# A two-layer hybrid decoder trunk: the first modulation in eight blocks instead of four, constants in three transfers, tiles 4 to 7 modulated in pairs

## The chip, the cores and the metric

The kernel runs on one core of a Trainium2 chip. The metric is the device time of one execution in microseconds (us). The engines are named as in the profile: PE is TensorE, ACT is ScalarE, DVE is VectorE, POOL is GpSimd, SP is SyncE, whose queue issues most of the DMAs. In the timeline an engine's name with a q (SPq) means that the row is an issue.

## The reference

```python
def hybrid_layer(x, c_act, ...):                       # x: 1024 tokens x 1024, two layers
    mod = c_act @ w_mod + b_mod                        # one row of 3072
    shift, scale, gate = jnp.split(mod[:, None, :], 3, axis=-1)
    h = rms_norm(x, pre_gain) * (1.0 + scale) + shift
    proj = h @ w_in                                    # 3088 columns
    (aq, ak, av, ag, rq, rk, rv, rg, gq, gk, gv, gg, ga) = jnp.split(proj, IN_SPLITS, axis=-1)
    ...                                                # windowed attention, retention, gated linear attention
    y = jnp.concatenate([a_out, r_out, g_out], axis=-1) @ w_out
    return x + gate * rms_norm(y, post_gain)
```

with `c_act = silu(c)`. What matters here is the start of layer 0: `shift` and `scale` are sums over 1024 rows of an 8 MB part of `w_mod`, every normalised token row is scaled by `gain = pre_gain * (1 + scale)` and moved by `shift`, and only then can the first projection begin.

## The kernel before

The tokens are 8 tiles of 128. `hT[(l, p)]` holds the modulated, transposed activations of the pair p of tiles in two halves of an fp32 value (a high part, rounded to fp32r, and the remainder), so each projection is three passes: high by high, high by low, low by high. Weights are split in the same way: a `Paced` load has `issue()` (a DMA of 256 KB into one of five stage buffers `st`) and `convert()` (high part on ACT, low part on POOL or DVE). The places of weights and activations lie in two areas, `arena0` and `arena1`.

`first_stage` is written out by hand, and all five engines follow its order (`manual_schedule`). It does the following for tiles 0 to 3:

- It loads `c`, the identity `ident`, `freq` (frequencies for the rotary tables), the bias rows, the four x tiles `xe`, and `w_m0`, the part of `w_mod` for shift and scale, into `wm` in the space of `arena1`, together with the first projection weights `gg` and `rg`.
- It normalises each tile: sum of squares on ACT (L731), scale and power on DVE and POOL (`rstd_of`, L604, L607), scaling on DVE (L745). `tables` is a chain of DVE steps for the rotary tables, of which `more(n)` places the next n.
- `spin(n)` issues n matmuls of the identity by itself, whose result is not used.
- In each of 4 rounds s, two blocks of 128 features are handled. `turn(s)` transposes the two blocks of the four tiles into two PSUM banks and sums 8 chunks of `wm[:, s]` weighted with `c_act` into the bank `pm`, on four 32-row strips. ACT copies the sums (`row`, L782), four small matmuls with `sel` add the strips and turn them into columns of `pc`, DVE makes `gain` and `shift` (L790 to L792), ACT modulates one block and DVE the other (L799 to L803), and DVE takes the remainders (L806).
- `products(s - 1, ...)` multiplies the blocks of the round before by `gg`, 24 matmuls of 272 columns into the four accumulators `acc`; some of them stand ahead of the columns of round s, the rest behind the modulation.
- After the last round come `rg`'s four conversions, into `arena1`, and the 24 products of blocks 6 and 7. Then x of tiles 4 to 7 is loaded in half tiles into buffers `kept`.

Everything after is ordered by a planner for PE: jobs (generators) yield delays from the table `L` or flags, the clock `clk` counts an estimated cost of each matmul, and `pump()` steps the jobs that are due between chunks of projection matmuls. The other engines' orders are set by when their instructions are recorded. Tiles 4 to 7 are jobs of `pre_first`, one for each tile: after the delays `pf3` and `pf2` they take squares (L621), scale (L637), wait `pre1`, and then for each half tile transpose four blocks into an `aux` bank, modulate each with its own instruction of 128 columns (L651 on ACT, L653 on DVE), and split (L657, L658). The projections `rg` of tiles 0 to 3 run meanwhile (`mm` banks); tanh copies of the gates are L1079, and the low-rank gate inputs of the gated linear attention are transposed one tile at a time and copied by L1097.

There are 3 PSUM banks with the tag `mm` and 5 with the tag `aux`; the four `acc` and `pm` hold the five.

Of the kernel before, what the change touches and what calls it, by code (L numbers as in the profile page):

```python
# [10 lines left out]
F32 = mybir.dt.float32  # L11
# [49 lines left out]
def host_constants():  # L61
    f = np.float32
    c = {}
    c["ident"] = np.eye(P, dtype=f)
# [4 lines left out]
    c["freq"] = np.broadcast_to(freq, (P, 64)).copy()  # L69
    c["causal"] = (i[:, None] <= i[None, :]).astype(f)  # L70
    c["mask2"] = ((i[:, None] <= i[None, :]) & (i[:, None] // 32 == i[None, :] // 32)).astype(np.int32)
    c["curmask"] = (i[:, None] >= i[None, :]).astype(np.int32)
    gam = 1.0 - 2.0 ** (-5.0 - np.arange(4, dtype=np.float64))
    c["reps"] = (4.0 * EPS * gam[None, :] ** (-2.0 * (i[:, None] + 1.0))).astype(f)
    c["vdec"] = (gam[None, :] ** (-(i[:, None] + 1.0))).astype(f)
# [4 lines left out]
    c["cdt"] = cdt  # L80
    c["ones"] = np.ones((P, 4), f)
    r = np.ones((P, 256), f)
    r[:, ::32] = 0.0
    c["rmask"] = r
    c["hmask"] = (i[:, None] // 32 == np.arange(4)[None, :]).astype(f)
# [8 lines left out]
def trunk(ctx: ExitStack, tc: tile.TileContext, ins, cst, out):  # L94
# [153 lines left out]
    ident = cload("ident", eng=A)  # L248
# [227 lines left out]
    def load(l, name, first=None):  # L476
# [10 lines left out]
        def conv(kc, st):  # L487
# [5 lines left out]
            else:  # L493
# [4 lines left out]
                e = G if first == "AG" or name[0] == "o" and kc == 2 else eng(f"wlo{kc}")  # L498
# [125 lines left out]
    def pre(l, t, xt, xn=None):  # L624
# [7 lines left out]
        xn = xn or junk  # L632
# [28 lines left out]
    def pre_first(t, xt):  # L661
        yield L["pf3"] + L["pf2"] * (t - 4)
        yield from pre(0, t, xt, xt)
# [10 lines left out]
    def first_stage():  # L674
# [3 lines left out]
        freq = cload("freq", eng=A)  # L678
# [10 lines left out]
        wm = bp.tile([P, 4 * SLOT], F32, tag="arena1", name="wm").rearrange("p (s k n) -> p s k n", s=4, k=KT)  # L689
        gg, rg = load(0, "gg", "AG"), load(0, "rg", "AV")  # L690

        def wm_load(s):
            for i in range(2):
                nc.sync.dma_start(wm[:, s, 4 * i:4 * i + 4], w_m0[s, :, 4 * i:4 * i + 4])

        for s in range(3):
            gg.issue()
            wm_load(s)
# [18 lines left out]
        spin(6)  # L717
        V.tensor_copy(posf, pr[:, 0:8])
        more(3)
        A.activation(th0, c_nat, AF.Tanh, scale=0.5)  # L720
        V.scalar_tensor_tensor(c_act, th0, 1.0, c_nat, ALU.add, ALU.mult)
        V.tensor_scalar(c_act, c_act, 0.5, None, ALU.mult)
        pr = mm()
        transp(pr[:, 0:24], rows, ident[0:24, 0:24])
        spin(18)
        rc = small(24)
        base = small(8)
        sel = small(1)
        for t in range(4):
            ss = small(1)  # L730
            A.activation(wm[:, 3, 2 * (t % 2):2 * (t % 2) + 2].rearrange("p k n -> p (k n)"), xe[t], AF.Square, accum_out=ss)  # L731
            r = rstd_of(ss, 1, 1.0 / D, EPS)
            if t == 0:
                more(1)
            elif t == 1:
                V.tensor_copy(rc, pr[:, 0:24])
                V.tensor_scalar(base, rc[:, 8:16], 1.0, None, ALU.add)
                V.tensor_reduce(sel, ident[:, 0:97:32], AX.X, ALU.add)
                more(1)
            elif t == 2:  # L740
                more(1)
            else:
                A.activation(w[:, 0, :, 256:272], low, AF.Copy)
                V.tensor_tensor(w[:, 1, :, 256:272], low, f(w[:, 0, :, 256:272]), ALU.subtract)
            V.tensor_scalar(xe[t], xe[t], r, None, ALU.mult)  # L745
        gg.convert()
        gg.issue()
        wm_load(3)
        for _ in range(4):
            rg.issue()  # L750
        for p in range(2):
            hT[(0, p)] = place(TOK[0][p])

        def product(t, b, x, y, start, stop):
            h = hT[(0, t // 2)]
            mult(acc[t][:, 0:272], h[:, x, b, (t % 2) * P:(t % 2) * P + P], w[:, y, b, 0:272], start, stop)

        def products(s, ts):
            for t in ts:
                for b in (2 * s, 2 * s + 1):  # L760
                    for x, y in ((0, 0), (0, 1), (1, 0)):
# [1081 lines left out]
```

## Time and profile before

| | us |
|---|---|
| median of 3 runs (984.5 to 988.84) | 985.13 |
| the profiled execution | 987.97 |
| its span, first to last instruction | 986.0 |
| PE busy in the span | 963.0 |
| DVE, ACT, POOL busy | 682.5, 396.2, 246.2 |
| mean granted clock of PE | 0.993 |

A row of a stretch (`10.00:20.00 ...`) gives its length, then for each of PE, PEld, DVE, ACT and POOL the busy time with the number of instructions, then the granted PE clock (1.00 is full), the share of the DMA engines and GB/s. A stretch asked for PE alone has only PE's busy time. A row of the timeline gives the start, the length, the engine, the line of the kernel, the operation, destination and sources with their shapes, how many follow each other, and in brackets how long the engine stood idle before it and what released it. A matmul of fp32 data is two records, one of fp32r data is one; so 16 records of 128x512 in `aux<-wm,c_act` are 8 sums, and 8 records of `mm<-sm,t` are 4 columns.

### The profile page before, as it was taken

Reading aid. Unit: us, or ns where it says so; the run is one execution under the profiler, and the core shown is the slowest. Engines: PE = TensorE matmul, PEld = TensorE weight load, DVE = VectorE, ACT = ScalarE, POOL = GpSimd, SP = SyncE. Lnnn points to the kernel's source line nnn. Section 1 sums busy time; section 2 is a strip of 40 time slices with the busy share of each in tenths; the row PEclk is TensorE's granted clock in tenths of the full one; section 3 lists DMA queues with packets and bytes.
Section 4 is the critical chain, followed back from the end, with each engine's and each line's share of the span. In section 5 each row is a group of like instructions: output and inputs, shape, how many; then the busy total and the mean of one; then the engine's idle time right before and its main releaser. Section 6 shows DMA issues by size and latency. Waiting matters only on the chain. (4 is left out here: it accounts for less than half of the span.)

```text
span 986.0 us, 19571 instructions
## 1 busy us (share of the span) xinstructions
PE 963.0 (98%) x7184; PEld 830.4 (84%) x7184; DVE 682.5 (69%) x1602; ACT 396.2 (40%) x1114; POOL 246.2 (25%) x310
## 2 busy tenths in 40 slices
PE   6999999999999999999999999999999999999996
PEld 4789999989997777778889999998999877777775
DVE  6476868777766787754697376785765577676885
ACT  3475301233322656633365321133333256664231
POOL 2321101233320324420124010123322034545000
PEclk9999999999999999999999999999999999999999
DMA  9745614542225254597665131352122334488783
GB/s 347 272 118 164 220 33 140 154 125 92 86 85 153 92 182 156 161 299 238 211 201 177 49 97 39 112 147 69 52 96 86 129 91 124 121 264 278 247 269 125
DMA packets 108735, 150.33 MB, mean 152 GB/s; under 512 B 12088, under 2 KB 59740, under 8 KB 107616
## 3 DMA queue, kind: packets, MB, share of 16 engines
q1 hardware_dynamic: 97200, 134.75, 43.4%
q10 hardware_dynamic: 11440, 14.34, 4.0%
q8 instruction: 56, 0.92, 0.4%
q14 instruction: 39, 0.32, 0.1%
HBM read 110.25 MB, written 36.70 MB: 149 GB/s over the span
## 5 line engine op out<-in xcount | busy, mean ns | idle before, releaser
L172 PE MATMUL mm<-arena,arena 128*128 128x256 f32 (+2 forms) x1824 | 298.7, 317 | 0.5 <-DVE t L1260 0.3
L172 PE MATMUL mm<-arena 128*128 128x256 f32 (+2 forms) x1728 | 284.8, 318 | 0.0
L172 PEld LDWEIGHTS mm<-arena,arena 128*128 128x128 f32 x1824 | 253.5, 190 | 26.1 <-issue 4.8
L172 PEld LDWEIGHTS mm<-arena 128*128 128x128 f32 x1728 | 240.4, 189 | 24.3 <-issue 4.2
L607 POOL TENSOR_TENSOR sm<-sm,mhalf 128x1 f32<-128x1 f32 (+1 forms) x64 | 57.6, 900 | 295.0 <-DVE sm L604 159.1
L172 PE MATMUL mm<-arena,mx 128*128 128x512 f32 (+1 forms) x564 | 130.9, 388 | 0.3 <-DVE t L1461 0.3
L172 PEld LDWEIGHTS mm<-arena,mx 128*128 128x128 f32 x564 | 101.5, 188 | 24.5 <-issue 1.5
L156 ACT ACTIVATE t<-aux 128x256 f32<-128x256 f32 (+2 forms) x124 | 52.4, 437 | 94.7 <-PE aux L187 78.2
L156 ACT ACTIVATE arena<-st 128x512 fp32r<-128x512 f32 x94 | 56.2, 628 | 47.5 <-PE mm L172 19.2
L499 POOL TENSOR_TENSOR arena<-st,arena 128x512 fp32r<-128x512 f32 x31 | 44.9, 1448 | 106.8 <-ACT arena L156 60.9
L1018 POOL TENSOR_TENSOR smx<-smx,sm 128x512 f32<-128x512 f32 x32 | 35.0, 1095 | 132.7 <-DVE sm L1017 115.9
L499 DVE TENSOR_TENSOR arena<-st,arena 128x512 fp32r<-128x512 f32 x77 | 61.5, 821 | 5.3 <-ACT arena L156 3.7
L1014 ACT ACTIVATE smx<-smx,sm 128x129 f32<-128x129 f32 x128 | 49.9, 393 | 31.3 <-DVE sm L1011 31.3
L318 DVE SCALAR_TENSOR_TENSOR acc<-ms,c_act,acc 128x512 f32<-128x512 f32 x60 | 46.3, 772 | 14.8 <-DMA ms<-in_w_mod_dram 14.1
L1062 ACT ACTIVATE t<-aux 128x256 f32<-128x256 f32 x32 | 12.2, 382 | 77.6 <-PE aux L172 70.2
L172 PEld LDWEIGHTS aux<-t,mx 32*128 32x128 f32 (+1 forms) x896 | 39.8, 187 | 3.8 <-issue 1.7
L172 PE MATMUL aux<-t,mx 32*128 32x32 f32 (+1 forms) x896 | 40.9, 272 | 0.0
L1009 DVE COPY_PREDICATED smx<-c_curmask,aux 128x256 f32<-128x256 int32 x64 | 25.2, 445 | 17.4 <-ACT smx L156 14.8
L1364 DVE SCALAR_TENSOR_TENSOR t<-t,sm,t 128x512 f32<-128x512 f32 x32 | 24.3, 781 | 18.2 <-DMA t<-in_x_dram 8.7
L187 PE MATMUL aux<-c_ident,t 128*128 128x128 f32 x186 | 32.9, 277 | 1.5 <-ACT t L1194 0.9
L172 PEld LDWEIGHTS aux<-kT,mx 64*128 64x128 f32 x384 | 24.6, 185 | 10.9 <-issue 6.3
L1067 DVE TENSOR_TENSOR t<-aux,sm 128x256 f32<-128x256 f32 x32 | 13.6, 425 | 27.3 <-POOL sm L607 27.3
(260 smaller groups left out, 1431.7 us busy)
## 6 DMA issues: line engine op xcount, KB each, us to landing
st<-in_w_in_dram SPq DMA_DIRECT2D x96, 256.0 KB, 3.7
ms<-in_w_mod_dram SPq DMA_DIRECT2D x64, 256.0 KB, 3.7
mx<-mixS SPq DMA_DIRECT2D x20, 512.0 KB, 5.4
st<-in_w_last_dram SPq DMA_DIRECT2D x36, 256.0 KB, 3.4
wm<-in_w_m_dram SPq DMA_DIRECT2D x8, 1024.0 KB, 11.3
mixS<-t SPq DMA_DIRECT2D x40, 128.0 KB, 2.0
t<-in_x_dram SPq DMA_DIRECT2D x18, 256.0 KB, 5.1
mixS<-t ACTq DMA_DIRECT2D x32, 128.0 KB, 2.1
```

Of the source, the lines that this page charges most:

```text
L156: A.activation(dst, src, AF.Copy)
L172: T.matmul(dst, lhsT, rhs, start=start, stop=stop)
L187: T.transpose(dst, src, idn)
L318: V.scalar_tensor_tensor(acc, wt, c_act[:, k:k + 1], acc, ALU.mult, ALU.add)
L499: e.tensor_tensor(lo, st, f(hi), ALU.subtract)
L607: G.tensor_tensor(r, r, mhalf[:, :w], ALU.pow)
L1009: V.copy_predicated(sv, curmask.unsqueeze(1).to_broadcast((P, 2, P)), pv[:, :, n // P - 1, :])
L1014: A.activation(sm[:, h, :], sm[:, h, :], AF.Exp, bias=mx[:, h:h + 1], accum_out=sums[:, h:h + 1])
L1018: eng("pn").tensor_tensor(sm[:, :, 0:128], sm[:, :, 0:128], rs.unsqueeze(2).to_broadcast((P, 4, P)), ALU.mult)
L1062: A.activation(sq, po, AF.Square)
L1067: V.tensor_tensor(h4(g1), h4(po), r.unsqueeze(2).to_broadcast((P, 4, 64)), ALU.mult)
L1364: V.scalar_tensor_tensor(xt[j], yg[j], r, xt[j], ALU.mult, ALU.add)
```

## The change

- **Constants.** `ident` and `freq` come as one transfer `early`; the nine later constants as two, `late` and `masks`; the small gate weights with 4 transfers instead of 8.
- **First stage.** `w_m0` is laid out in 8 blocks of 128 features (256 columns, shift and scale) and loaded a block at a time, one block ahead of the first `gg` load. Each of 8 rounds b sums 256 columns into one half of `pm`, transposes block b + 1, makes two columns, `gain` and `shift` of one block with two DVE instructions, and modulates the block (ACT in even rounds, DVE in odd ones, both in the last). In round b the products of block b - 1 stand behind everything else. `gg` is converted in even rounds, the `rg` loads are issued in rounds 0 and 2, two of `rg`'s conversions move ahead of the last modulation. The spins are 8 and 12 instead of 6, 18 and 6; the table steps are spread anew.
- **Tiles 4 to 7.** `norm` takes the squares and scales; it runs for tiles 4 and 5 at the end of `first_stage`. `pre_pair` handles two tiles at a time: in each of four steps two blocks of both tiles go into one bank, are modulated with instructions of 256 columns (DVE in even steps, ACT in odd ones) and split for the pair. The table `L` gets `pf4@2`, `pf4@3`, `pf5` and a new `pf3`.
- The low part of two of `rg`'s chunks goes to POOL instead of DVE.

On DVE, around the norms of tiles 0 to 3, before (`mx_141` is the table chain's buffer, `xk` and `mx_107` are the x tiles, the `sm` are small columns):

```order
L718 COPY sm_92<-mm_132 128x8
L364 TENSOR_TENSOR mx_141<-sm_92,c_freq 128x512
L367 TENSOR_SCALAR mx_141<-mx_141 128x512
L369 TENSOR_SCALAR mx_141<-mx_141 128x512
L721 SCALAR_TENSOR_TENSOR c_act<-sm_79,sm_72 128x8
L722 TENSOR_SCALAR c_act<-c_act 128x8
L604 TENSOR_SCALAR sm_173<-sm_171 128x1
L372 SCALAR_TENSOR_TENSOR mx_141<-mx_141 128x512
L745 TENSOR_SCALAR xk_105<-xk_105,sm_173 128x1024
L604 TENSOR_SCALAR sm_180<-sm_178 128x1
```

and after:

```order
L750 COPY sm_92<-mm_129 128x8
L363 TENSOR_TENSOR mx_141<-sm_92,c_early 128x512
L366 TENSOR_SCALAR mx_141<-mx_141 128x512
L368 TENSOR_SCALAR mx_141<-mx_141 128x512
L753 SCALAR_TENSOR_TENSOR c_act<-sm_79,sm_72 128x8
L754 TENSOR_SCALAR c_act<-c_act 128x8
L371 SCALAR_TENSOR_TENSOR mx_141<-mx_141 128x512 x2
L762 TENSOR_REDUCE sm_165<-c_early 128x1
L603 TENSOR_SCALAR sm_169<-sm_167 128x1
L371 SCALAR_TENSOR_TENSOR mx_141<-mx_141 128x512
L772 TENSOR_SCALAR xk_103<-xk_103,sm_169 128x1024
L603 TENSOR_SCALAR sm_176<-sm_174 128x1
```

The first table step reads `c_early` in place of `c_freq`, and two more table steps stand ahead of the first norm.

On PE, one round of before (the third; `mm_332` and `mm_333` take the transposes, `mm_217` is `pc`, `aux_125` to `aux_128` are the accumulators):

```order
L187 MATMUL mm_332<-c_ident,mx_107 128x128 x2
L187 MATMUL mm_333<-c_ident,xk_105 128x128
L187 MATMUL mm_333<-c_ident,xk_106 128x128
L187 MATMUL mm_333<-c_ident,mx_107 128x128 x2
L172 MATMUL aux_129<-wm,c_act 32x512 x8
L172 MATMUL aux_125<-arena_71 128x272 x6
L172 MATMUL mm_217<-sm_170,t_53_354 128x1 x4
L172 MATMUL aux_126<-arena_71 128x272 x6
L172 MATMUL aux_127<-arena_71 128x272 x6
L172 MATMUL aux_128<-arena_71 128x272 x6
```

and one round after (`mm_205` is `pc`, `aux_122` to `aux_125` are the accumulators):

```order
L170 MATMUL aux_126<-wm,c_act 32x256 x8
L185 MATMUL mm_333<-c_early,xk_103 128x128
L185 MATMUL mm_333<-c_early,xk_104 128x128
L185 MATMUL mm_333<-c_early,mx_105 128x128 x2
L170 MATMUL mm_205<-sm_165,t_49_331 128x1 x2
L170 MATMUL aux_122<-arena_71 128x272 x3
L170 MATMUL aux_123<-arena_71 128x272 x3
L170 MATMUL aux_124<-arena_71 128x272 x3
L170 MATMUL aux_125<-arena_71 128x272 x3
```

The transposes of the next block now stand between the sums and the columns, and all products behind the columns.

On ACT, behind the conversions of `rg` (`arena_459` and `arena_479` are `arena1`), before:

```order
L495 ACTIVATE arena_459<-st_215 128x512
L1087 ACTIVATE sm_546<-aux_125 128x16
L1079 ACTIVATE t_75_551<-aux_125 128x256
L1087 ACTIVATE sm_556<-aux_126 128x16
L1079 ACTIVATE t_79_561<-aux_126 128x256
L1087 ACTIVATE sm_566<-aux_127 128x16
L1087 ACTIVATE sm_576<-aux_128 128x16
L621 ACTIVATE t_90_594,sm_596<-xl_492 128x512
```

and after:

```order
L494 ACTIVATE arena_479<-st_304 128x512
L620 ACTIVATE t_71_539,sm_540<-xl_523 128x512
L620 ACTIVATE t_71_539,sm_540<-xl_524 128x512
L620 ACTIVATE t_75_550,sm_551<-xl_525 128x512
L620 ACTIVATE t_75_550,sm_551<-ms_526 128x512
L1118 ACTIVATE sm_581<-aux_122 128x16
L1110 ACTIVATE t_83_586<-aux_122 128x256
L1118 ACTIVATE sm_591<-aux_123 128x16
```

Four squares of x now stand ahead of the first evacuation of an accumulator.

The diff, cut to its core (the line numbers of after are two lower than before's in the helpers and about 30 higher behind the first stage):

```diff
-                e = G if first == "AG" or name[0] == "o" and kc == 2 else eng(f"wlo{kc}")
+                e = G if first == "AG" or name[0] == "o" and kc == 2 else eng(f"wlo{(3 if kc < 2 else 0) if first else kc}")
...
-    def pre_first(t, xt):
-        yield L["pf3"] + L["pf2"] * (t - 4)
-        yield from pre(0, t, xt, xt)
+    def norm(xt):
+        junk = t2()
+        r = rstd2(squares(xt, [junk, junk]))
+        for j in range(2):
+            V.tensor_scalar(xt[j], xt[j], r, None, ALU.mult)
+
+    def pre_pair(p, xs_):
+        h = hT[(0, p)] = place(TOK[0][p])
+        if p > 2:
+            yield L["pf3"]
+            for xt in xs_:
+                norm(xt)
+        yield L[f"pf4@{p}"]
+        for q in range(4):
+            x = aux()
+            hf = t2()
+            for i in range(2):
+                kb = 2 * q + i
+                for tt in range(2):
+                    c = 256 * i + P * tt
+                    transp(x[:, c:c + P], xs_[tt][kb // 4][:, (kb % 4) * P:(kb % 4) * P + P], ident)
+            for i in range(2):
+                kb, c = 2 * q + i, slice(256 * i, 256 * i + 256)
+                gain, shift = modc[(0, 1)][:, kb:kb + 1], modc[(0, 0)][:, kb:kb + 1]
+                if q % 2:
+                    A.activation(hf[:, c], x[:, c], AF.Identity, scale=gain, bias=shift)
+                else:
+                    V.tensor_scalar(hf[:, c], x[:, c], gain, shift, ALU.mult, ALU.add)
...
-        for s in range(3):
-            gg.issue()
-            wm_load(s)
+        for j in range(3):
+            wm_load(*((0,), (1, 2), (3, 4))[j])
+            gg.issue()
...
+        at = turn(0)
+        for b in range(KT):
+            half = pm[:, 256 * (b % 2):256 * (b % 2) + 256]
+            for k in range(KT):
+                g = k % 4
+                mult(half[32 * g:32 * g + 32, :], c_act[:, k:k + 1].to_broadcast((P, 32)), wm[:, b, k], k < 4, k > 3, 0.12)
+            row = t1()
+            A.activation(row, half, AF.Copy)
+            nxt = turn(b + 1) if b < KT - 1 else None
+            if b == KT - 1:
+                arenas.append(bp.tile([P, 4 * SLOT], F32R, tag="arena1", name="arena1"))
+                rg.convert()
+                rg.convert()
+            for i in range(2):
+                mult(pc[:, 2 * b + i:2 * b + i + 1], row[:, i * P:(i + 1) * P], sel, True, True)
+            V.scalar_tensor_tensor(gain[:, b:b + 1], pc[:, 2 * b + 1:2 * b + 2], base[:, b:b + 1], rc[:, 16 + b:17 + b],
+                                   ALU.add, ALU.mult)
+            V.tensor_tensor(shift[:, b:b + 1], pc[:, 2 * b:2 * b + 1], rc[:, b:b + 1], ALU.add)
...
+            at = nxt
...
+            if b:
+                for t in range(4):
+                    for x, y in ((0, 0), (0, 1), (1, 0)):
+                        product(t, b - 1, x, y)
...
+        for xt in late[:2]:
+            norm(xt)
...
-"pf3": 0.3, "pf2": 2.6,
+"pf3": 3.0, "pf4@2": 4.2, "pf4@3": 7.0, "pf5": 0.9,
```

More of the change, by code (lines that the diff above doesn't have):

```diff
@@ L747, in first_stage @@
+        V.tensor_tensor(w[:, 1, :, 256:272], low, f(w[:, 0, :, 256:272]), ALU.subtract)
+        more(2)
+        wm_load(5, 6)
         gg.issue()
-        wm_load(3)
-        for _ in range(4):
-            rg.issue()
+        wm_load(7)
         for p in range(2):
             hT[(0, p)] = place(TOK[0][p])
-        def product(t, b, x, y, start, stop):
-            h = hT[(0, t // 2)]
-            mult(acc[t][:, 0:272], h[:, x, b, (t % 2) * P:(t % 2) * P + P], w[:, y, b, 0:272], start, stop)
@@ L758, in products @@
[L758 to L761, printed above, removed]
[L762 to L772 removed]
+        hp = hT[(0, 0)], hT[(0, 1)]
@@ L814, in first_stage @@
+            if b == 0:
+                more(2)
+            elif b == 2:
                 more(1)
-            elif s == 1:
+            for x in parts:
+                remainder(*x)
+            at = nxt
+            if b == 0:
                 more(2)
-            elif s == 2:
+            elif b == 1:
+                more(1)
+            elif b == 3:
                 A.activation(th0, c_nat, AF.Tanh, scale=0.5)
-        arenas.append(bp.tile([P, 4 * SLOT], F32R, tag="arena1", name="arena1"))
```

179 lines of the change are left out of this document (80 added, 99 removed).

## The prediction, made before the changed kernel was run

> **What bounds the kernel now.** I read the busy totals first, then the 40 slices, then stretches of 10 us, then TensorE's own waits.
>
> ```profile
> PE 963.0 (98%) x7184; PEld 830.4 (84%) x7184; DVE 682.5 (69%) x1602; ACT 396.2 (40%) x1114; POOL 246.2 (25%) x310
> PE   6999999999999999999999999999999999999996
> 0.00:10.00 10.00, 5.22 (x22) 4.85 (x23) 2.56 (x10) 4.70 (x7) 1.65 (x11) 1.00 0.81 271
> 10.00:20.00 10.00, 7.37 (x53) 5.54 (x52) 8.40 (x19) 2.11 (x6) 4.01 (x5) 1.00 0.98 385
> 20.00:30.00 10.00, 7.64 (x44) 5.72 (x44) 5.22 (x11) 4.96 (x7) 3.50 (x2) 0.66 1.02 421
> 60.00:70.00 10.00, 7.73 (x57) 7.43 (x56) 6.10 (x16) 7.52 (x23) 2.14 (x4) 0.85 0.53 143
> PE aux L187 <- ACT t L651: 2.3, 1, 2.3
> ```
>
> TensorE (PE) is full from the second slice to the last. So work off its path is free, and whatever lets it reach its full stream earlier shortens the span one for one. Only two places stand open: the first stage (PE 5.22, 7.37 and 7.64 us busy of 10, with the granted clock at 0.66 in the third stretch) and 60 to 70 us, with one wait of 2.3 us for ScalarE (ACT). The diff touches just these two. The profiled execution took 987.97 us, 1.97 around its span of 986.0; it is 2.84 above the median of 985.13. I take the same number of microseconds off both.
>
> The stage as it runs now, rows of the timeline (start, length, engine):
>
> ```profile
> 8.14 6.34 PE L172 MATMUL aux<-c_ident 128*128 128x128 f32 x36
> 17.66 0.33 PE L187 MATMUL mm<-c_ident,mx 128*128 128x128 f32 x1 [2.21 <-DVE mx L745]
> 18.36 1.92 PE L172 MATMUL aux<-wm,c_act 128*32 128x512 f32 x16
> 42.24 0.38 PE L187 MATMUL mm<-c_ident,xk 128*128 128x128 f32 x2
> 42.90 0.38 PE L187 MATMUL mm<-c_ident,mx 128*128 128x128 f32 x2
> 45.92 0.98 PE L172 MATMUL mm<-sm,t 128*128 128x1 f32 x8
> 46.76 5.51 PE L172 MATMUL aux<-arena 128*128 128x272 f32 x42
> 52.11 9.54 PE L172 MATMUL mm<-arena,arena 128*128 128x256 f32 x79
> ```
>
> First sums at 18.36, last product done at 46.76 + 5.51 = 52.27, from then on projections without a gap. Unit prices at full clock: one 512-wide sum 1.92; a product 5.51 / 42 = 0.131; four column products 0.98; a pair of transposes (42.90 - 42.24) / 3 = 0.22, so 0.44 for four; a projection matmul 9.54 / 79 = 0.121.
>
> **Term 1, the first sums start earlier.** What holds the first transposes is the norm chain on VectorE (DVE), and what holds that is a table instruction standing ahead of it:
>
> ```profile
> 3.50 1.28 ACT L720 ACT_TABLE_LOAD   x1 [3.50 <-DMA c_ident<-cst_ident_dram]
> 7.78 0.69 DVE L364 TENSOR_TENSOR mx<-sm,c_freq 128x512 f32<-128x512 f32 x1 [4.10 <-DMA c_freq<-cst_freq_dram]
> 9.59 0.15 DVE L604 TENSOR_SCALAR sm<-sm 128x1 f32<-128x1 f32 x1
> 9.81 0.92 POOL L607 TENSOR_TENSOR sm<-sm,mhalf 128x1 f32<-128x1 f32 x1 [7.76 <-DVE sm L604]
> 10.77 0.75 DVE L745 TENSOR_SCALAR xk<-xk,sm 128x1024 f32<-128x1024 f32 x1 [0.44 <-POOL sm L607]
> 15.86 1.74 DVE L745 TENSOR_SCALAR mx<-mx,sm 128x1024 f32<-128x1024 f32 x1 [0.54 <-POOL sm L607]
> 10.47 1.06 ACT L731 ACTIVATE wm<-mx 128x1024 f32<-128x1024 f32 x1 [0.23 <-DMA mx<-in_x_dram]
> 11.44 0.19 ACT L731 ACTIVATION_READ_ACCUMULATOR wm<-mx 128x1 f32 x1
> ```
>
> The last sum of squares is ready at 11.63, yet the last tile is normalised at 15.86 + 1.74 = 17.60, since freq came at 7.78 and all DVE work stood behind it. With freq in the identity's transfer (there by 3.50) the three opening table instructions, 0.69 each at most, run from about 3.8 to 5.6 and c_act and two more to 7.2. The chain then follows the squares: tile 0 normalised at 9.4, tile 1 at 11.1, tile 2 at 12.7. For tile 3: the square at 11.63, DVE free at 12.75, scale 0.15, the power on GpSimd (POOL) about 0.7 with its handoffs (0.92 in the row, the first of four; DVE idles 0.44 and 0.54 for it), 0.75 for the scaling: 14.4. It takes 0.75 and not 1.74, because the POOL subtraction that ran beside it moves behind the first sums. Sums begin near 14.7: **3.7 us** gained. The spread: 0 if freq's larger transfer lands as late as 7.78 again, 4 if nothing waits.
>
> The first block of w_m0 must have landed. DMA moves 2.71 MB by 10 us (271 GB/s) and about 3.9 MB in each of the next tens. Four x tiles (2.1 MB) and one block (1.05) with the small constants are 3.35 MB, so about 11.7 plus a completion of about 1.4 (x tile 3 is 2.3 MB in and starts ACT at 10.47). Block 0 is there at 13.1, block 1 at 16.4, then one each 2.6 us, and block 7 near 33.5. The transfers' order on SP, with the stage loads between them, is the same kind as now, and no round below waits for one.
>
> **Term 2, rounds of half the size.** A round of before ties sums, row copy, columns, modulation and products into one chain, and twice PE waits in it. One round after has 8 sums of 256 columns (bounds 0.96 by width and 1.92 by count; I take 1.1, nearer to width, as the long row keeps PE streaming), 4 transposes 0.44, 2 column products 0.5 and 12 products 1.57: 3.6, with handoffs 3.7. The other engines' steps, from these rows:
>
> ```profile
> 20.35 0.60 ACT L782 ACTIVATE t<-aux 128x512 f32<-128x512 f32 x1 [8.00 <-PE aux L172]
> 22.86 0.78 ACT L802 ACTIVATE t<-mm,mod,mod 128x512 f32<-128x512 f32 x1 [1.92 <-DVE mod L792]
> 23.67 0.63 ACT L803 ACTIVATE arena<-t 128x512 fp32r<-128x512 f32 x1
> 22.68 0.15 DVE L792 TENSOR_TENSOR mod<-mm,sm 128x2 f32<-128x2 f32 x1
> 24.17 1.29 DVE L806 TENSOR_TENSOR arena<-t,arena 128x512 fp32r<-128x512 f32 x2
> ```
>
> Row copy of half width about 0.4 (between 0.39 for an evacuation of 256 columns, below, and 0.60), two small DVE steps 0.35, modulation 0.78, high part 0.63, remainder 0.65: 2.8 us after the row. Products lag one round, so this lies beside the next 3.7 us of PE. Row copy runs beside the 0.44 of transposes. Walk: sums 0 at 14.7 to 15.8; columns done 16.8; sums 1 to 17.9; the third turn waits for bank and ACT (row 1 stands behind modulation 0 and the high part), columns 1 done 19.6; products 0 to 21.2; five rounds of 3.7 to 39.7; the last one 1.1 + 0.4 + 0.5 + 24 x 0.131 = 5.2. End near 45.0, that is 30.3 us after the first sums against 52.27 - 18.36 = 33.9: **3.6 us** gained. The two rg stage copies that now stand ahead of the last modulation cost ACT 1.2, and 12 products of block 6 (1.57) cover most of that.
>
> **Term 3, tiles 4 to 7.**
>
> ```profile
> 65.15 0.63 ACT L621 ACTIVATE t<-t 128x512 f32<-128x512 f32 x1
> 65.67 0.20 ACT L621 ACTIVATION_READ_ACCUMULATOR t<-t 128x1 f32 x1
> 65.77 1.51 ACT L651 ACTIVATE t<-aux,mod,mod 128x128 f32<-128x128 f32 x4
> 67.13 0.28 ACT L1097 ACTIVATE gaT<-aux 48x128 fp32r<-48x128 f32 x1
> 67.33 1.11 PE L187 MATMUL aux<-c_ident,ms 128*128 128x128 f32 x4 [2.27 <-ACT t L651]
> 68.09 3.44 PE L172 MATMUL mm<-arena,arena 128*128 128x256 f32 x17
> 69.17 0.39 ACT L1079 ACTIVATE t<-mm 128x256 f32<-128x256 f32 x1 [0.75 <-issue]
> 67.00:68.00 1.00, 0.68 (x3) 0.55 0.27 42
> 71.00:72.00 1.00, 1.00 (x11) 1.00 0.51 186
> ```
>
> PE waits 2.27 for a PSUM bank that ACT empties at 67.28, and then runs 17 projections in 3.44 (0.202 each, not 0.121) on a clock of 0.55: 2.27 + 17 x 0.081 + 0.3 on transposes = 3.9 us lost. After, squares of tiles 4 and 5 stand ahead of ACT's other evacuations, and modulations are half as many and twice as wide. New wait: PE reaches the fourth gate transpose after 86 projections and 16 transposes, 86 x 0.121 + 1.8 = 12.2 us behind the stage's end, E. As built it shares the bank of the first, which ACT frees behind 8 squares (0.83 each), 7 tanh copies (0.39), 2 modulations (about 0.5 each), 3 stage copies and 2 high parts (about 0.6 each) and 5 small ones (0.2): 14.4 us, begun about 1.6 before E, so at E + 12.8. One more wait follows for the next bank (two modulations, about 1.0). I charge 1.8 of new waits without a drop of the clock, and gain **2.1 us**; bounds 0 (clock drops again) to 3.9.
>
> **Edits at nothing.** Constants in three transfers and gate weights in four instead of eight: fewer small issues on SP, all behind the late x loads; what hides them is the stage's own tail, and without that cover they would only hold back the first gate stores, which PE does not read. The late x loads themselves:
>
> ```profile
> 38.62 1.37 SPq L831 DMA_DIRECT2D xl<-in_x_dram  x3
> ```
>
> They stand behind the fourth rg load, which waits for a stage buffer that POOL frees with the third gg remainder. That one now comes in round 4, about 33, so x starts some 5 us earlier, as E does, and is there by about 41 (2.1 MB at some 400 GB/s), before its squares near 43. If it came 2 us later than that, PE would stall for the excess. The remaining planner order moves with its times; the slices behind the third are all at 9 but the last, so I give it 0 with 1.5 either way. Fewer spins (40 records against 60) lie ahead of the path. DMA bytes are the same.
>
> Sum: 3.7 + 3.6 + 2.1 = 9.4. Own time 987.97 - 9.4 = 978.6; median 985.13 - 9.4 = 975.7, forecast **976**.
>
> **Rivals.**
>
> (a) The clock drops in the first rounds. In before it did, and the sums, transposes and columns then took about twice as long:
>
> ```profile
> 22.00:23.00 1.00, 0.05 (x1) 0.86 0.98 412
> 28.00:29.00 1.00, 1.00 (x6) 0.50 1.03 406
> ```
>
> For it: the spins end earlier (24 records from about 8, at the 0.18 of the row at 8.14 until 12, sooner if the clock has risen) and PE then has only scattered transposes until 14.7, a gap of 2 to 4 us; 2.27 was enough at 65. Against: from 14.7 on the rounds leave no gap over 0.7. Doubling turn, sums and columns of rounds 0 and 1 and most of products 0 moves sums 2 from 21.2 to 24.9: 3.7 us, giving 979.7. [...]
>
> (b) The late tiles still stall and cool the clock: term 3 is lost, 978.
>
> [...]
>
> (d) The change doesn't bring the first sums forward (freq lands late again, or x3 is held by POOL): terms 2 and 3 alone, 979.4.
>
> (e) More: sums at 0.96 and no wait at the late tiles: 973.
>
> **Numbers.** Chances: forecast 0.37, (a) 0.28, (b) 0.12, (c) 0.05, (d) 0.06, (e) 0.12. Half a per cent, 4.9 us, is about what a measurement here can tell from no change; faster means below 980.2. That takes in the forecast, (b), (e) and over half of (a) and (d): 0.78. Same 0.16 (the rest of those, and (a) with (b) at 981.8), slower 0.06. Range 971.5 ((e) less 1.5 of planner order) to 982.5 ((a) with (b) and a little of that).
>
> **What would show it.** Term 1: first sums near 14.7 and the last xn scaling at 0.75. Term 2: sums of 256 columns near 1.1, rounds 3.7 apart, last product before 46. Term 3: waits of PE in the 20 us behind the stage under 2 us in total, clock 1.00. Wrong if the clock column shows 0.5 for more than 5 us behind the first sums, if PE waits there for wm, or if later stretches lose what the first gained.

## The result: 979.9 us, faster by 0.6%, and 3.9 us short of the forecast

| | before | after |
|---|---|---|
| median of 6 runs, us | 985.3 (984.5 to 988.84) | 979.91 (978.99 to 980.71) |
| the profiled execution: time, span | 987.97, 986.0 | 980.64, 978.5 |
| PE busy in the span | 963.0 | 958.2 |

The ratio is 0.9939, with a 95% interval of 0.9923 to 0.9955: 5.4 us. A second session gave the same changed kernel 0.9959 (0.9944 to 0.9975), 981.64 against 985.59. The forecast was 976.0, its range 971.5 to 982.5.

The page of the changed kernel, PE's totals and its 40 slices, and then five stretches (length, busy time of PE, PEld, DVE, ACT, POOL, granted PE clock, DMA share, GB/s):

```profile
PE 958.2 (98%) x7228; PEld 825.8 (84%) x7228; DVE 678.2 (69%) x1598; ACT 395.6 (40%) x1112; POOL 247.7 (25%) x311
PE   7999999999999999999999999999999999999996
0.00:10.00 10.00, 6.74 (x41) 6.45 (x42) 5.68 (x18) 5.50 (x9) 2.70 (x11) 1.00 0.82 298
10.00:20.00 10.00, 6.74 (x53) 3.82 (x52) 6.38 (x15) 3.54 (x9) 2.79 (x3) 0.83 0.99 384
20.00:30.00 10.00, 10.00 (x100) 7.90 (x104) 7.04 (x17) 6.46 (x10) 3.66 (x2) 1.00 1.02 414
60.00:70.00 10.00, 9.61 (x80) 9.61 (x81) 9.69 (x21) 8.81 (x21) 2.76 (x2) 1.00 0.68 210
100.00:110.00 10.00, 8.58 (x74) 8.38 (x73) 8.43 (x19) 2.79 (x4) 0.00 (x0) 1.00 0.49 141
```

The third stretch is full (PE 10.00, before 7.64) and 60 to 70 nearly so (9.61, before 7.73). The stretch of 100 to 110 has a hole, 8.58; in the kernel before, where the same work stood some 7 us later, PE was busy 9.78 of the 10 us from 108 to 118. The timeline of the stage and of that place, rows of DVE, PE and POOL:

```profile
3.77 0.69 DVE L363 TENSOR_TENSOR mx<-sm,c_early 128x512 f32<-128x512 f32 x1
13.09 0.75 DVE L772 TENSOR_SCALAR mx<-mx,sm 128x1024 f32<-128x1024 f32 x1 [0.44 <-POOL sm L606]
14.15 1.93 PE L170 MATMUL aux<-wm,c_act 128*32 128x256 f32 x16
22.01 1.07 PE L170 MATMUL aux<-wm,c_act 128*32 128x256 f32 x16
25.73 1.07 PE L170 MATMUL aux<-wm,c_act 128*32 128x256 f32 x16
42.22 0.61 PE L170 MATMUL mm<-sm,t 128*128 128x1 f32 x4 [0.51 <-ACT t L813]
42.77 2.53 POOL L498 TENSOR_TENSOR arena<-st,arena 128x512 fp32r<-128x512 f32 x2 [0.58 <-ACT arena L494]
43.78 0.55 DVE L800 TENSOR_SCALAR t<-mm,mod,mod 128x256 f32<-128x256 f32 x1 [0.63 <-ACT t L797]
44.36 1.08 DVE L801 CAST arena<-t 128x256 fp32r<-128x256 f32 x1
45.36 0.75 DVE L804 TENSOR_TENSOR arena<-t,arena 128x256 fp32r<-128x256 f32 x2
45.49 1.52 PE L170 MATMUL aux<-arena 128*128 128x272 f32 x10 [0.73 <-DVE arena L801]
60.39 0.33 PE L185 MATMUL aux<-c_early,ms 128*128 128x128 f32 x1 [0.54 <-ACT t L686]
71.11 0.40 PE L170 MATMUL aux<-gaT,gwt 128*128 128x512 f32 x1
100.88 0.41 DVE L156 CAST arena<-st 128x512 fp32r<-128x512 f32 x1
101.43 4.80 PE L170 MATMUL mm<-arena,arena 128*128 128x256 f32 x38 [1.42 <-DVE arena L156]
107.11 0.39 PE L170 MATMUL aux<-gaT,gwt 128*128 128x512 f32 x1
```

First sums at 14.15 (18.36 before), rounds 25.73 - 22.01 = 3.72 apart, last product done at 45.49 + 1.52 = 47.01 (52.27). PE's last two waits in the stage are 0.51, for the copy of the last sums, and 0.73, for a cast of 1.08 that runs beside POOL's conversions. The late tiles cost waits of 0.24 and 0.54, 0.78 in all. At 101.43 PE waits 1.42 for a weight conversion (of `rv`, a 512-wide cast) that stands on DVE behind the rotary's multiplications.

Two products with the gate weights (`aux<-gaT,gwt`, one each, 71.11 and 107.11) stand in every variant, so the span falls into five parts that can be compared. Each row is one profile, so one execution. "Half" is where PE's clock column was under 1.00 within the stage, read in stretches of 2 us. The rows below the first two are the experiments, which the next section explains by these names.

| profile | first sums | sums to last product | to gate product 1 | to gate product 2 | to the end | span | half |
|---|---|---|---|---|---|---|---|
| before | 18.36 | 33.91 | 27.65 | 34.23 | 871.85 | 986.0 | 22-30 |
| after | 14.15 | 32.86 | 24.10 | 36.00 | 871.39 | 978.5 | 14-18 |
| after_again | 14.18 | 32.83 | 24.10 | 37.86 | 873.83 | 982.8 | 14-18 |
| late_freq | 17.89 | 33.73 | 24.10 | 35.90 | 871.78 | 983.4 | 14-26 |
| after_no_pairs | 14.51 | 32.61 | 26.29 | 34.70 | 871.59 | 979.7 | 12-18 |
| spin_none | 14.43 | 34.69 | 24.07 | 35.98 | 870.83 | 980.0 | see below |
| tail | 14.59 | 34.61 | 24.09 | 35.97 | 873.64 | 982.9 | 13-24 |
| rv_act | 14.18 | 31.74 | 24.09 | 35.70 | 870.99 | 976.7 | none |
| best8 | 14.15 | 31.79 | 24.08 | 35.55 | 870.43 | 976.0 | none |
| early_only | 15.15 | 33.94 | 27.66 | 34.27 | 875.78 | 986.8 | 18-28 |
| pairs_only | 17.32 | 31.17 | 23.48 | 38.46 | 871.87 | 982.3 | none |
| early_pairs | 15.35 | 32.73 | 23.50 | 38.63 | 873.79 | 984.0 | 20-26 |
| fill4 | 15.64 | 29.84 | 26.20 | 34.16 | 872.86 | 978.7 | none |
| best4 | 16.18 | 29.81 | 23.54 | 38.42 | 872.05 | 980.0 | none |

Before to after: 4.21 + 1.05 + 3.55 - 1.77 + 0.46 = 7.5, the difference of the spans. One execution's profile is not exact to the last us: pairs_only has the instructions of before up to the first sums and began them at 17.32, not 18.36, and the four kernels with four rounds and early frequencies began them between 15.15 and 16.18.

### The profile page after: what moved, and what is told of

It reads as the page before. It is cut to its first block, busy times and chain, and to the rows that moved or that the text cites. A ratio compares the mean times of both kernels' runs of the same rounds, so it can differ in the third digit from the quotient of the medians.

```text
span 978.5 us, 19647 instructions
## 1 busy us (share of the span) xinstructions
PE 958.2 (98%) x7228; PEld 825.8 (84%) x7228; DVE 678.2 (69%) x1598; ACT 395.6 (40%) x1112; POOL 247.7 (25%) x311
## 4 chain that ended last, share of the span: by engine, by line
PE 89%; DVE 6%; DMA 1%; POOL 1%; issue 1%; ACT 1%; SPq 0%; POOLq 0%; DVEq 0%; ACTq 0%
PE mm L170 67%; PE aux L170 18%; PE aux L185 4%; POOL sm L606 1%; DMA ms<-in_w_mod_dram 1%; DMA t<-in_x_dram 0%; DVE t L1288 0%; DVE t L1290 0%; SPq L866 0%; PE mm L185 0%; DVE t L1179 0%; POOL mx L1211 0%; DVE acc L317 0%; DVE t L1099 0%; DVE t L1291 0%
## 5 line engine op out<-in xcount | busy, mean ns | idle before, releaser
L498 DVE TENSOR_TENSOR arena<-st,arena 128x512 fp32r<-128x512 f32 x76 | 59.2, 799 | 3.1 <-ACT arena L154 1.6
L1040 DVE COPY_PREDICATED smx<-c_masks,aux 128x256 f32<-128x256 int32 x64 | 25.3, 446 | 17.9 <-ACT smx L154 14.5
L185 PE MATMUL aux<-c_early,t 128*128 128x128 f32 x186 | 33.8, 277 | 1.5 <-ACT t L1225 0.9
```

The lines of the kernel that those rows point to most:

```text
L185: T.transpose(dst, src, idn)
L498: e.tensor_tensor(lo, st, f(hi), ALU.subtract)
L1040: V.copy_predicated(sv, curmask.unsqueeze(1).to_broadcast((P, 2, P)), pv[:, :, n // P - 1, :])
```

## The experiments

### The parts of the change alone

The frequencies beside the identity, in the kernel before (early_only):

```diff
-    c["ident"] = np.eye(P, dtype=f)
-    c["freq"] = np.broadcast_to(freq, (P, 64)).copy()
+    c["early"] = np.concatenate([ident, np.broadcast_to(freq, (P, 64))], 1)
...
-    ident = cload("ident", eng=A)
+    early = cload("early", eng=A)
+    ident, freq = early[:, 0:P], early[:, P:P + 64]
...
-        freq = cload("freq", eng=A)
```

> The kernel of before with one edit: ident and freq come in one transfer. Theory (the norm chain on DVE stood behind the table step that waited for freq): the wait of 4.1 us for freq is gone, the first 512-wide sums start near 15.3 instead of 18.36, the last product of the stage is done near 49 instead of 52.27, and the time falls by 2 to 3.5 us to about 982. Rival (the four large rounds bound the stage, so an earlier start is given back in them, by a cold clock or a wait for w_m0): the first sums are earlier, but the last product stays within 1 us of 52.3 and the time above 984.

Measured: 982.14 (981.16 to 988.81), ratio 0.9951 (0.9935 to 0.9967), as the theory had it. By the intervals, this one transfer can't be told from the whole change (0.9939 and 0.9959). PE's timeline:

```profile
43.58 5.51 PE L172 MATMUL aux<-arena 128*128 128x272 f32 x42
64.15 1.11 PE L187 MATMUL aux<-c_early,ms 128*128 128x128 f32 x4 [2.27 <-ACT t L652]
```

First sums at 15.15, last product at 49.09, both 3.2 earlier than before; the wait of 2.27 for the late tiles stays. The profiled execution was this kernel's slowest (986.8 of span), from the last part.

The pairs alone, in the kernel before (pairs_only), and both together (early_pairs):

```diff
-    def pre_first(t, xt):
...
+    def norm(xt):
+    def pre_pair(p, xs_):
...
-"pf3": 0.3, "pf2": 2.6,
+"pf3": 3.0, "pf4@2": 4.2, "pf4@3": 7.0, "pf5": 0.9,
```

> The kernel of before with tiles 4 to 7 modulated in pairs and tiles 4 and 5 normalised at the end of the first stage. Theory: PE's wait of 2.27 us behind the modulations and the half clock after it go, waits in the 20 us behind the stage stay under 1 us, and the time falls by about 3.5 us to about 982. Rival (the wait only moves to another bank and the clock falls again, or later slices give it back): under 1.5 us, time above 983.8.

> The kernel of before with both: freq beside ident, and the pairs; the first modulation keeps its four rounds. Theory (the eight rounds brought about 1 us of the whole): the parts add, 979 to 981, within 1.5 us of the changed kernel's 979.9. Rival (the eight rounds carry the gain, since they keep PE fed and warm): 982.5 or more.

Measured: pairs_only 986.97, ratio 1.0005 (0.999 to 1.0019); early_pairs 985.43, ratio 0.9984 (0.9968 to 1.0). Both theories missed: the pairs bring nothing here, and early_pairs is 3.3 us slower than early_only, not within 1.5 us of the changed kernel. Rows of pairs_only, PE and DVE:

```profile
17.32 1.92 PE L172 MATMUL aux<-wm,c_act 128*32 128x512 f32 x16
42.98 5.51 PE L172 MATMUL aux<-arena 128*128 128x272 f32 x42
98.67 0.69 DVE L1300 TENSOR_TENSOR rq<-t,t 128x512 f32<-128x512 f32 x1
99.28 0.68 DVE L499 TENSOR_TENSOR arena<-st,arena 128x512 fp32r<-128x512 f32 x1
100.02 4.97 PE L172 MATMUL mm<-arena 128*128 128x256 f32 x28 [2.45 <-DVE arena L499]
```

The table shows why: the way to gate product 1 shrinks from 27.65 to 23.48, by 4.17, and the way from there to gate product 2 grows from 34.23 to 38.46, by 4.23. PE reaches the next weights before DVE has made their remainder, which stands behind the rotary's steps; it waits 2.45, and 28 projections then take 4.97 (0.178 each, against 0.121), the clock being 0.84 from 100 to 110. The same rows show something else: the four-round stage, not touched in this kernel, took 31.17 and not 33.91, and its clock stayed full.

The changed kernel without its pairs (after_no_pairs; the diff is the one above, reversed):

> The changed kernel with the pairs undone (one job for each of tiles 4 to 7 as before, no norm in the first stage). Theory: PE waits again for ACT's modulations behind the stage, 2 to 4 us with the clock, and the time is 982.5 to 984. Rival (the pairs only moved a wait): within 1 us of 979.9.

Measured: 983.69, ratio 0.9968 (0.9953 to 0.9983). The wait of 2.27 is back:

```profile
62.23 0.66 PE L185 MATMUL aux<-c_early,ms 128*128 128x128 f32 x4 [2.27 <-ACT t L650]
```

In the eight-round kernel the pairs gain 26.29 - 24.10 = 2.2 at their place and lose 36.00 - 34.70 = 1.3 behind it. About 0.9 is left in these profiles. The intervals of the ratios touch (0.9923 to 0.9955 for the changed kernel in one session) or overlap (0.9944 to 0.9975 in the other), so a gain by the pairs is not shown in the time.

The changed kernel with freq in a transfer of its own again (late_freq; the diff of early_only, reversed):

> The changed kernel with one edit undone: the frequencies come in a transfer of their own behind the first ones again, all else (eight rounds, pairs) stays. Theory (the frequencies' transfer is what gains): the first table step on DVE goes from 3.77 back to about 7.8, the scaling of the last tile from 13.09 to about 16, first sums from 14.15 to 16.5 to 17.5, the last product ends 2.4 to 3.4 later than 47.0, and the time rises by as much, to about 983.5. Rival (the gain of the first stage is the eight rounds'): the first sums are late, and the time stays within 1 of the changed kernel.

Measured: 986.43 (983.94 to 988.95), ratio 0.9996 (0.9981 to 1.0012): no faster than the kernel before. Rows of DVE and PE:

```profile
7.35 0.69 DVE L363 TENSOR_TENSOR mx<-sm,c_freq 128x512 f32<-128x512 f32 x1 [3.64 <-DMA c_freq<-cst_freq_dram]
16.68 0.76 DVE L773 TENSOR_SCALAR mx<-mx,sm 128x1024 f32<-128x1024 f32 x1 [0.44 <-POOL sm L606]
17.89 1.94 PE L171 MATMUL aux<-wm,c_act 128*32 128x256 f32 x16
50.10 1.52 PE L171 MATMUL aux<-arena 128*128 128x272 f32 x10 [0.74 <-DVE arena L802]
```

First sums 17.89 - 14.15 = 3.74 later, last product 4.6 later, more than the 2.4 to 3.4 expected; the half clock was longer in this profile (14-26). The rival, that the eight rounds gain the first stage's time by themselves, falls.

### What the clock does in the stage

The changed kernel once more (after_again; no edit):

> The changed kernel once more, beside the variants that follow, and a second profile of the same code. If the place of the half clock is a matter of each execution, as the four-round stage suggests (its last product ended at 52.27 in one profile and at 48.49 in another, with no edit there), the half clock stands at another place or is absent (the first profile had it from 14.4 to 17.6), and the end of the last product moves by at most 1 us from 47.0, since the rounds are 3.73 apart by the other engines. If the phase is fixed by the code, sums 0 takes 1.93 again and the last product ends at 47.0 within 0.2. The time: 980 with 1 either way, ratio to the kernel before 0.9925 to 0.9955.

Measured: 981.64 (978.73 to 984.87). The same half clock stood at the same place, and the last product at 47.01 again; the profiled execution, 984.87, was long for other reasons (a wait of 1.8 at 101 and a clock of 0.83 behind it, and 2.4 in the last part). So two profiles alone did not show the phase to change. Two others with the same instructions up to that point do: rv_act kept the full clock, tail had 0.50 from 14 until 22 and later. The rows of the clock, after (all engines):

```profile
14.00:15.00 1.00, 1.00 (x9) 0.43 (x13) 0.97 (x3) 0.00 (x0) 0.00 (x0) 0.58 1.03 434
17.00:18.00 1.00, 1.00 (x13) 0.90 (x16) 0.22 (x3) 0.06 (x1) 0.86 (x1) 0.71 0.94 379
```

and tail (PE's busy time alone, then the clock):

```profile
16.00:17.00 1.00, 1.00 (x11) 0.50 0.98 418
20.00:22.00 2.00, 2.00 (x13) 0.50 0.98 414
22.00:24.00 2.00, 2.00 (x11) 0.57 1.01 406
```

From first sums to last product that is 31.74 without a drop (rv_act), 32.86 with 3.4 us of half clock (after: from 14.16 to 17.58, reckoned from the 0.58 and the 0.71), 34.61 with some 9 (tail: from the first sums at 14.59 to 23.72, reckoned from the 0.57). So the half clock came, and ended, at other moments under instructions that are the same up to the last round. What sets its moment is not shown here.

Without the twenty throwaway products ahead of the sums (spin_none):

```diff
-        spin(8)
...
-        spin(12)
```

> The changed kernel without the twenty throwaway products ahead of the first sums. Theory (they warm TensorE's clock): the granted clock is 0.5 from 14 to at least 18 and up to 21.5, sums 0 and sums 1 take about 1.9 to 2.1, and the last product ends 0.5 to 2.5 later than 47.0. Rival (the rounds have slack, since they are bound by the other engines at 3.73 apiece): the sums are slow, and the last product still ends within 0.5 of 47.0; the time is that of the changed kernel within 0.7.

Measured: 982.08 (980.83 to 983.27), ratio 0.9965 (0.9951 to 0.9979). A row of PE's timeline and one of the clock:

```profile
14.43 1.94 PE L170 MATMUL aux<-wm,c_act 128*32 128x256 f32 x16
16.00:17.00 1.00, 1.00 (x8) 1.00 1.00 418
```

The sums of rounds 0 and 1 took 1.94 and 1.93, the last product ended at 49.12: 2.1 later than 47.01, as the theory had it, and the rounds have no slack to take it up, since PE is busy without a break from 20 to 40. The clock column shows 1.00 all along, though these sums took nearly twice the 1.07 of later ones. In the time the loss doesn't show: 982.08 can't be told from the changed kernel's 981.64 in the same session, as the rival had it.

### What the end of the stage waits for

The last round's halves in two tiles of their own, and `rg`'s conversions behind the modulation (tail):

```diff
-                rg.convert()
-                rg.convert()
             for i in range(2):
...
             hf = t2()
             if b == KT - 1:
-                parts = [[hp[i][:, a:a + 1, b, 0:256] for a in range(2)] + [hf[:, 256 * i:256 * i + 256]] for i in range(2)]
+                hs = hf, t2()
+                parts = [[hp[i][:, a:a + 1, b, 0:256] for a in range(2)] + [hs[i][:, 0:256]] for i in range(2)]
...
-        rg.convert()
-        rg.convert()
+        for _ in range(4):
+            rg.convert()
```

> The changed kernel with its last round's two halves in two tiles of their own, and the rg weights' conversions behind the last modulation instead of ahead of it. Theory (the tail's end is DVE's chain, held up by ACT over a shared tile, 0.63, and by POOL's work beside the 128x256 cast, 1.08 where 0.43 would do): the last product ends at 46.0 to 46.3 instead of 47.0, the time falls by 0.5 to 1.0. Rival (PE then waits for the rg weights): PE waits for arena behind 50, 0.5 to 1.5, and the time stays or rises by 0.5.

Measured: 983.37, ratio 0.9974 (0.9963 to 0.9986), no gain. From the last sums to the last product 6.33 us (42.87 to 49.20), against 6.36 in the changed kernel. DVE, POOL, and PE's last wait:

```profile
46.00 0.54 DVE L800 TENSOR_SCALAR t<-mm,mod,mod 128x256 f32<-128x256 f32 x1 [0.63 <-ACT t L797]
46.58 0.29 DVE L801 CAST arena<-t 128x256 fp32r<-128x256 f32 x1
46.79 1.85 DVE L804 TENSOR_TENSOR arena<-t,arena 128x256 fp32r<-128x256 f32 x2
47.02 2.77 POOL L498 TENSOR_TENSOR arena<-st,arena 128x512 fp32r<-128x512 f32 x2 [2.60 <-DMA t<-in_gla_gate_b_dram]
48.69 0.51 PE L170 MATMUL aux<-arena 128*128 128x272 f32 x2 [0.50 <-DVE arena L804]
```

The cast fell from 1.08 to 0.29 and the two remainders rose from 0.75 to 1.85: the slow DVE casts and remainders are those beside POOL's conversions (47.02 to 49.79 here, 42.77 to 45.30 in after). The change itself put these there: in the changed kernel POOL makes the remainders of rg's first two chunks and DVE those of the last two, where before POOL made only the fourth and DVE the first three. The tail profile's longer stage is its half clock. The wait of 0.63 for ACT stayed, with no tile written by both, so the shared tile was not its cause. Both also read one PSUM bank, and in after DVE's modulation began at 43.78, behind ACT's of 43.19 + 0.56. In the kernel before, the last round's two blocks lay in two banks and ACT's and DVE's modulations began together, at 47.40; so I take the shared bank for the likely reason, but it was not tried.

### The place at 101

The first cast of the `rv` weights on ACT, which in after is busy 1.95 us from 95 to 100 and 0.00 from 100 to 105 (rv_act):

```diff
-                if first:
+                if first or l == 0 and name == "rv":
                     A.activation(hi, st, AF.Copy)
```

> The changed kernel with one cast (the first chunk of the rv weights) on ACT instead of on DVE behind the rotary. Theory (the late tiles' gain is partly given back at that cast): the PE wait of 1.42 at 101.43 goes to under 0.4, and the time falls by 1.0 to 1.4, to about 978.7. Rival 1 (the next DVE work in the row, the remainders of the same weights, is then late): PE waits there for arena line 498 with 0.5 to 1.2, and the time falls by less than 0.7. Rival 2 (the gain is absorbed further on, as before): the milestones behind 107 stand earlier, and the end does not move.

Measured: 980.03 (978.82 to 982.83), ratio 0.9949 (0.9932 to 0.9965), not to be told from the changed kernel beside it (0.9959). Rows of PE and DVE:

```profile
44.40 1.52 PE L170 MATMUL aux<-arena 128*128 128x272 f32 x10 [0.73 <-DVE arena L801]
100.46 1.88 DVE L498 TENSOR_TENSOR arena<-st,arena 128x512 fp32r<-128x512 f32 x3
101.20 3.62 PE L170 MATMUL mm<-arena,arena 128*128 128x256 f32 x22 [0.38 <-DVE arena L498]
```

The wait of 1.42 became 0.38, for the next DVE step of the same weights; the part between the gate products fell by 0.30 only. The wait went as in the theory, the gain stayed under 0.7 as in rival 1. Of the span's 1.8 less than after's, 1.1 is the stage's clock.

### What is left of the eight rounds

Four rounds with the frequencies early, and their throwaway products moved into a wait (fill4, against early_only):

```diff
             at = [mm(), mm()]
+            if s == 1:
+                spin(6)
             for i in range(2):
...
-            if s == 1:
-                spin(6)
```

> The kernel before with the frequencies beside the identity, and with its six throwaway products of the second round moved from behind that round's transposes to ahead of them, where PE waits 1.65 for a bank. Theory (eight rounds are worth nothing at the same clock: from the first sums to the last product four rounds took 31.2 and eight 31.7, both at full clock; 33.9 for four rounds was at half clock in part): the products (1.50 warm) vanish in the wait, the clock stays 1.00, and the last product ends 29.7 to 30.3 after the first sums, at about 45.2, ahead of the eight rounds' 47.0; the time is 1.5 to 3.5 below that of the frequencies' edit alone, some 980.5. Rival (eight rounds are what keeps TensorE busy): the clock drops all the same, the last product ends at 48 or later, and the time is that of the frequencies' edit alone, 982, within 1.

Measured: 980.79 (979.6 to 983.98), ratio 0.994 (0.9917 to 0.9962). PE:

```profile
15.64 1.92 PE L172 MATMUL aux<-wm,c_act 128*32 128x512 f32 x16
19.19 1.58 PE L172 MATMUL aux<-c_early 128*128 128x128 f32 x12
39.97 5.51 PE L172 MATMUL aux<-arena 128*128 128x272 f32 x42
```

The throwaway products vanish in the wait, the clock is full, and the last product ends at 45.48, 29.84 after the first sums. With one transfer and one moved line, without eight rounds and without pairs, this kernel's ratio is that of the whole change (0.9939). The theory's stage and time held. A gain over early_only (0.9951) is not shown, since the intervals overlap. Nor is it shown that the products keep the clock: four rounds with them at the old place had a half clock in three profiles and a full one in one (pairs_only), with them in the wait a full one in two (fill4, best4).

The same with the pairs and the `rv` cast on ACT (best4):

> The same four rounds with the frequencies early and the throwaway products in the wait, and with tiles 4 to 7 in pairs and the rv weights' first cast on ACT. Theory: last product at about 45.2; the pairs' gain of 4.2 (27.65 to 23.48 from the last product to the first gate product) stays, and of the 2.45 that PE waited for the rv weights 1.2 to 2.4 goes; the time is 977 to 979, not slower than the eight rounds with the same repair. Rival (the wait for the rv weights is for loads, not for DVE): PE waits 2 or more near 100 again, the clock drops behind it, time 981 or more.

Measured: 981.86 (980.27 to 987.26), ratio 0.9951 (0.9934 to 0.9967): the rival's time, by another cause. DVE and PE:

```profile
96.24 0.69 DVE L1300 TENSOR_TENSOR rq<-t,t 128x512 f32<-128x512 f32 x1
96.85 0.69 DVE L500 TENSOR_TENSOR arena<-st,arena 128x512 fp32r<-128x512 f32 x1
97.59 4.91 PE L172 MATMUL mm<-arena 128*128 128x256 f32 x28 [2.45 <-DVE arena L500]
```

The cast that I moved was not the one waited for. It is a remainder of the weights ahead of `rv` (L500), directly behind the rotary; 2.45, and a clock of 0.86 from 90 to 100, as in pairs_only. The pairs' gain is lost again.

The changed kernel with that cast on ACT and 20 throwaway products instead of 12 (best8, the diff of rv_act and this):

```diff
-        spin(12)
+        spin(20)
```

> The changed kernel with the rv weights' first cast on ACT, and twenty throwaway products instead of twelve ahead of the first transposes. Theory (an idle TensorE before the first sums lets the clock drop in most executions: the half clock stood from 14.4 to 17.6 in three profiles with this code, to 22.7 in one, and nowhere in one): the products run to 12.3 to 13.3, the clock is 1.00 from 14 on, sums 0 takes 1.07, the last product ends at 45.7 to 46.3 as in the one profile without the drop (45.92); PE wait at 101 under 0.5; the time is 978.3 with 1 either way. Rival (the drop doesn't depend on it): half clock in the first rounds again, last product at 47.0 or later, time about 980.

Measured: 978.23 (977.96 to 980.52), ratio 0.9915 (0.9893 to 0.9938), the fastest of all here; 987.39 for the kernel before in that session. The changed kernel was not timed in it, and its interval of the first session overlaps, so a gain over it (1.7 by the medians) is possible and not shown. PE, and the clock:

```profile
7.39 4.79 PE L170 MATMUL aux<-c_early 128*128 128x128 f32 x40
14.15 1.07 PE L170 MATMUL aux<-wm,c_act 128*32 128x256 f32 x16
14.00:16.00 2.00, 2.00 (x24) 1.00 1.02 430
44.41 1.53 PE L170 MATMUL aux<-arena 128*128 128x272 f32 x10 [0.74 <-DVE arena L801]
```

PE is busy to 12.18, the clock stays full, and the last product ends at 45.94, without delaying the first sums. One profile can't prove that the drop is gone for good: rv_act, with 12 products, had a full clock too. Six runs within 2.6 us, four of them within 0.4, speak for it.

## Why the prediction was right in sign and 3.9 us too low

**Term 1, first sums earlier (3.7): held.** 4.21 in the profiles, and 3.74 by undoing the one transfer. The mechanism is as told: the table step at 3.77, the last scaling at 13.09 in 0.75 and not 1.74. In before POOL's subtraction ran beside it, from 15.79 to 17.05; in after it starts at 17.14. In early_only, with POOL's subtraction in its old place, the transfer alone gave 3.2; fill4 and best4, which have it there too, show that scaling at 1.75.

**Term 2, rounds of half the size (3.6): this step failed.** The rounds themselves came out as worked (3.72 against 3.7, sums 1.07 against 1.1). What was wrong is what they were set against: "30.3 us after the first sums against 52.27 - 18.36 = 33.9". The 33.9 held some 2.7 us lost to half clock (33.91 - 31.17), which I read as the price of four rounds; at full clock four rounds take 31.2 (pairs_only), 1.5 of it throwaway products, and 29.8 with those in the wait (fill4, best4). Eight rounds take 31.7 at full clock (rv_act; 31.8 in best8), 30.3 + 1.4: the last round took 6.4 and not my 5.2, by the waits of 0.51 and 0.73 in it. So at the same clock the profiles show no gain by eight rounds. I had quoted the clock's 0.50 between 22 and 30 and used it only in a rival about the kernel after; it also had to be taken out of the kernel before.

**Term 3, the late tiles (2.1): bigger at its place, and then half given back.** 3.55 at the place (waits of 0.78 in all instead of the 1.8 charged), 1.77 of it lost before the next gate product. That leaves 1.78, near the 2.1, but by two errors that offset each other. The remaining planner order, put at 0 with 1.5 either way, was the term that missed it: PE arrived at `rv`'s conversion sooner than DVE. In four rounds the same wait with its half clock ate the whole of it.

**Rival (a), the clock drops in the first rounds (0.28): it came.** Priced at 3.7, it measured 1.1 in the profiles of after and after_again (32.86 and 32.83 against 31.74) and 2.9 in that of tail (34.61). 979.7 is close to the time that came, but that is luck: it came by 1.1 of clock, a term 2 that had shrunk, and 1.8 given back. That 2.27 us of idle time are enough for a drop holds for two profiles and not for two others: 17 projections behind that wait took 3.44 in before and 3.43 in early_only, 2.36 in after_no_pairs and 2.35 in fill4. (b), (d) and (e) did not come: the clock behind the late tiles was 1.00, freq came early (the table step at 3.77), and the sums took 1.07 and not 0.96. Nor did the slower outcome: in the stage the clock was full from 18 on.

By the profiles of before and after the gain was 7.5, against the 9.4 of the sum: terms 1, 2 and 3 came to 4.21, 1.05 and 1.78, the last part to 0.46. By the medians it was 5.4 and 4.0. The profiled execution of before lay 2.7 above its median, and I took the same microseconds off both; part of what a profile of one execution shows is that execution's.

**Open:** the last 871 us differ from 870.4 to 875.8 between profiles, with nothing changed there but what planner times shift. Single waits and half clocks differ (PE's wait for one rotary step between 600 and 700 is 0.5 in best8, 1.3 in after, 1.7 in after_again); what sets them was not settled.

## What to carry to other kernels

Before a stage's length is set against a new design, take out the time that the clock was low in it: compare the price of one full-clock instruction (0.131 a product here, 0.224 for tail's first 12, most of them at half clock) with the same form in the stage. Where the first big block waits for a chain of small steps, look for the load at the head of that chain; one moved transfer had about the whole gain (early_only 0.9951), and the change without it none (late_freq 0.9996). A gain at one place counts only if the other engines are ready at the next: lay the two milestones behind it side by side before believing it (pairs_only: 4.17 gained to the first, 4.23 lost to the second).

## What the hardware showed that I had not expected

- The same instructions up to 14 us ran the next rounds with 0, 3.4 or about 9 us of half clock (rv_act, after, tail), a spread of 2.9 us in the stage (31.74, 32.86, 34.61).
- With the throwaway products in a wait the stage took 29.84 (fill4), with them behind it 31.17 (pairs_only); by themselves they took 1.58 and 1.50. With 20 instead of 12 of them ahead of the first sums, ending at 12.18 (best8) instead of 10.3 (after), the clock was full in the one profile taken, though 1.26 of idle time still followed.
- The granted-clock column read 1.00 in spin_none while sums took 1.94 instead of 1.07; the duration of a known form told more than the column.
- DVE operations of one form took 0.29 or 1.08 (cast, 128x256; tail, after) and 0.37 or 0.92 each (remainder; after, tail), with POOL's conversions running beside the long ones.
